# Two projections of a decoder layer turned round: tokens stationary, 512 weight columns moving, and the residual in token rows

## The chip, the cores and the metric

The kernel runs on one core of a Trainium2 chip. The metric is the device time in microseconds of one execution; the time of a kernel is the median of its runs. A core has a matrix engine (TensorE), three engines for elementwise work (VectorE, ScalarE, GpSimd) and a queue engine (SyncE) from which most transfers are issued. TensorE holds up to 128x128 numbers of one operand (the stationary one, loaded by a "weight load") and streams the columns of the other (the moving one) past them; sums are formed in PSUM, in accumulators of 128 rows by up to 512 numbers.

## The reference

One step of a decoder layer for 256 prompt tokens and 8x8 sample tokens, 320 tokens in all, in float32. D = 2048 channels, FF = 5632.

```python
def decoder_layer(x, ...):
    z = rms_norm(x, g_mix) @ w_in
    # z is cut into a gated short convolution (B, C, h), q, k, v and two gates
    ...
    merged = sigmoid(gate_c) * y_conv + sigmoid(gate_a) * y_attn
    h = x + merged @ w_o
    hn = rms_norm(h, g_ffn)
    h = h + (silu(hn @ w_gate) * (hn @ w_up)) @ w_down
    return h, ...
y_prompt, y_sample = rms_norm(hp, g_final), rms_norm(hs, g_final)
```

The change touches `merged @ w_o`, the residual, both norms behind it and `... @ w_down`. The projections w_in, w_conv_out, w_attn_out, w_gate and w_up and the attention stay as they are, up to the form in which their results are handed on.

## The kernel before, in words

**Products in three parts.** TensorE's faster float32 type (fp32r in the rows, printed as f32 in the matmul rows) keeps fewer bits, so each operand is split exactly into a high and a low part, and a product is three matmuls: high weight with high x, high weight with low x, low weight with high x. `load_cols` (L96 to L107) brings a weight tile of four contraction chunks (128 each) by 256 output columns, 512 KB, on SyncE's queue into one of four raw buffers; `split_to` (L92) makes the high part on ScalarE (L93, Copy) and the low part on VectorE (L94, a subtraction), into three buffers each. `product` (L116 to L141) takes these tiles: for two output chunks of 128 channels it holds two accumulators [128 channels, 320 tokens] and issues, for each contraction chunk and output chunk, three matmuls with 128x128 weights stationary and the 320 tokens moving (L132). So everything is kept in [channel, token] form. At the end of each weight tile, `tick()` issues a step of side work (attention, norm pieces) between the matmuls, and what stands in `pending`.

**Order.** Instructions are written in program order and a scheduler puts them in one stream for each engine; `after(...)` forces what is issued in it behind given instructions. Each engine then runs its own stream in order and waits on semaphores.

**Start.** x is loaded in three tiles of token rows (`xs`: 128, 128 and 64 tokens by 2048). `x_prep` (L237 to L250) transposes one chunk of 128 channels with three TensorE transposes (L240; the third is 64 rows by 64), makes the split operands `xh_t` and `xl_t` scaled by g_mix, and copies the chunk to `hT`, the residual in [channel, token] form: 12 such copies on ScalarE (L250), four on VectorE (L248). This stands between the first product, k and v (tile kv). The squares of x are summed from the token rows; `start_rest` (L298 on) spreads the norm's factor (r3, one number for a token) over all 128 rows by a diagonal matrix and a matmul with ones (tile prb, L305; plain float32, two passes each).

**Output projection and second norm (L791 to L831).** Eight products with w_o (tile wo, operands m_h and m_l): each result chunk is added to hT, split into hh_t and hl_t scaled by g_ffn, and its squares are summed on GpSimd into `hacc` (L806 to L810). Behind the first gate product (tile fg) a matmul of ones with hacc (pss2, L830) sums over the channels, and the factor rb2 [128, 320] is worked out from it.

**SwiGLU and down projection (L834 to L891).** FF is worked in two halves, of 24 and 20 chunks. Each half: products with w_gate and w_up (tiles fg, fu), their merge split into a_h and a_l, then eight products with w_down over the half's chunks (tile dn), added to hT (L872). In the second half six transposes behind each product (L878) bring the two finished chunks into token rows, ScalarE sums their squares (L883) and `y_part` (L860) multiplies them by g_final.

**End (L893 to L915).** The last chunk's sum completes the sum of squares, `inv_root` (ScalarE's square root, L181, and a Newton step on VectorE) gives the factor of all three token blocks at once, the rows are scaled in pieces on VectorE and ScalarE, and seven transfers on SyncE's queue write them. A dummy square root (L863) stands ahead of half 1's dn products.

**Tables.** ScalarE loads a table when it changes between kinds of function (ACT_TABLE_LOAD in the rows), Sigmoid and Sqrt among them.

Of the kernel before, what the change touches and what calls it, by code (L numbers as in the profile page):

```python
# [15 lines left out]
D = 2048  # L16
# [24 lines left out]
def hybrid_layer(ctx: ExitStack, tc: tile.TileContext, a: dict, o: list):  # L41
# [50 lines left out]
    def split_to(hi, lo, src):  # L92
        last["hi"] = nc.scalar.activation(hi, src, AF.Copy)  # L93
        last["lo"] = nc.vector.tensor_sub(lo, src, hi.bitcast(F32))  # L94

# [20 lines left out]
    def product(load, nk, xh, xl, name, tiles=None, loaded=None, before=None):  # L116
        """Two output chunks: psum[c][128, T] = sum over nk contraction chunks."""
# [24 lines left out]

    def flip(ap):
# [33 lines left out]
    def inv_root(v, shape, name, pool, out=None):  # L177
        """v ** -0.5, one Newton step on the table's root."""
        s = pool.tile(shape, F32, tag=f"rs_s{shape[1]}", name=u(name))
        r = pool.tile(shape, F32, tag=f"rs_r{shape[1]}", name=u(name))  # L180
# [11 lines left out]
    hT = xp.tile([P, KC, T], F32, name="hT")  # L192
# [22 lines left out]
    xs = [st.tile([P, D], F32, name=f"x{t}") for t in range(3)]  # L215
# [11 lines left out]
    # activity for the PE's clock gate while x is on its way  # L227
# [9 lines left out]
    def x_prep(kc):  # L237
# [9 lines left out]
        if kc % 4 == 3:  # L247
            nc.vector.tensor_copy(hT[:, kc, :], pt[:, :T])  # L248
        else:
            nc.scalar.activation(hT[:, kc, :], pt[:, :T], AF.Copy)  # L250
# [46 lines left out]

    def start_rest():  # L298
        yield
        yield  # L300
        prb = ps_aux("prb")
        for t, (t0, tn) in enumerate(TOK):
            dg = st.tile([P, P], F32, name=f"dg{t}")
            nc.vector.tensor_scalar(dg[:tn, :tn], ident[:tn, :tn], r3[:tn, t:t + 1], None, op0=ALU.mult)
            nc.tensor.matmul(prb[:, t0:t0 + tn], ones[:tn, :], dg[:tn, :tn], start=True, stop=True)  # L305
        nc.vector.tensor_copy(rb, prb[:, :T])
# [90 lines left out]
    def prompt_scores(kv, gp, bias):  # L397
        """Two heads of a kv group; a row of s is [block 0 | block 1 over both key blocks]."""
# [326 lines left out]
    mp_ = ExitStack()  # L725
    mm = mp_.enter_context(tc.tile_pool(name="mm", bufs=1, side="right"))
    m_h = mm.tile([P, KC, T], F32R, name="m_h")
    m_l = mm.tile([P, KC, T], F32R, name="m_l")
    n18 = mm.tile([2 + 2 * NB, DC], F32, name="n18")

    def conv_state():
        for h in range(2):
# [3 lines left out]
            nc.vector.tensor_copy(n18[:, h * 512:(h + 1) * 512], pg[:18, :])  # L736
# [22 lines left out]
    for mp in range(8):  # L759
# [18 lines left out]
        for c in range(2):  # L778
# [3 lines left out]
            split_to(m_h[:, mp * 2 + c, :], m_l[:, mp * 2 + c, :], t)  # L782

# [1 line left out]
    yp.close()  # L785
    hp = ctx.enter_context(tc.tile_pool(name="hp", bufs=1))
    hacc = hp.tile([P, T], F32, name="hacc")
# [3 lines left out]
    for mp in range(8):  # L791
        c0 = mp * CW
        ps = product(
            lambda k0, n: load_cols(w_o, k0, n, c0), KC,
            lambda k: m_h[:, k, :], lambda k: m_l[:, k, :], "wo",
        )
        for c in range(2):
            k = mp * 2 + c
            nc.vector.tensor_add(hT[:, k, :], ps[c][:, :T], hT[:, k, :])
            nc.scalar.activation(hh_t[:, k, :], hT[:, k, :], AF.Copy, scale=g_ffn[:, k:k + 1])  # L800
            nc.vector.scalar_tensor_tensor(
                hl_t[:, k, :], hT[:, k, :], g_ffn[:, k:k + 1], hh_t[:, k, :].bitcast(F32),
                op0=ALU.mult, op1=ALU.subtract,
            )
            if k == 0:
                nc.gpsimd.tensor_tensor(hacc, hT[:, k, :], hT[:, k, :], op=ALU.mult)  # L806
            else:
                t = tmp("tc", "sq")[:, :T]
                nc.gpsimd.tensor_tensor(t, hT[:, k, :], hT[:, k, :], op=ALU.mult)
                nc.gpsimd.tensor_tensor(hacc, hacc, t, op=ALU.add)  # L810
    mp_.close()

# [4 lines left out]
    for half in range(2):  # L817
        f0 = 0 if half == 0 else FH[0]
        nf = FH[half]
        a_h = fp.tile([P, FH[0], T], F32R, tag="ah", name=u("a_h"))  # L820
        a_l = fp.tile([P, FH[0], T], F32R, tag="al", name=u("a_l"))
        for fpair in range(nf // 2):
            c0 = (f0 + fpair * 2) * P
            psg = product(
                lambda k0, n: load_cols(w_g, k0, n, c0), KC,
                lambda k: hh_t[:, k, :], lambda k: hl_t[:, k, :], "fg",
            )
            if half == 0 and fpair == 0:
                pss = ps_aux("pss2")
                nc.tensor.matmul(pss[:, :T], ones, hacc, start=True, stop=True)  # L830
                rstd_of(pss[:, :T], [P, T], "r2", hp, out=rb2)  # L831
            gs = []
            for c in range(2):
                t, t2 = tmp("ta", "gs")[:, :T], tmp("tb", "sg")[:, :T]  # L834
                nc.vector.tensor_mul(t, psg[c][:, :T], rb2)
                nc.scalar.activation(t2, t, AF.Sigmoid)
# [7 lines left out]
            for c in range(2):  # L844
                nc.vector.tensor_mul(gs[c], psu[c][:, :T], gs[c])
                split_to(a_h[:, fpair * 2 + c, :], a_l[:, fpair * 2 + c, :], gs[c])
        if half == 1:
            ya = xp.tile([P, 2, D], F32, tag="xh", name="ya")
            yb = xp.tile([P, 2, D], F32, tag="xl", name="yb")
            y_sb = [ya[:, 0, :], ya[:, 1, :], yb[:, 0, :]]  # L850
            gfb = yb[:, 1, :]
            nc.gpsimd.dma_start(gfb, a["g_final"].partition_broadcast(P))
            ssf = op.tile([P, 3, KC], F32, name="ssf")
            nc.vector.memset(ssf, 1.0)
            s15 = op.tile([P, 3], F32, name="s15")

            def y_part(k, pt):
                for t, (t0, tn) in enumerate(TOK):
                    ks = slice(k * P, (k + 1) * P)
                    nc.vector.tensor_mul(y_sb[t][:tn, ks], pt[:tn, t * P:(t + 1) * P], gfb[:tn, ks])  # L860

            warm = op.tile([P, 1], F32, name="warm")
            nc.scalar.activation(warm, ones[:, 0:1], AF.Sqrt)  # L863
        for mp in range(8):
            c0 = mp * CW
            ps = product(
                lambda k0, n: load_cols(w_d, f0 + k0, n, c0), nf,
                lambda k: a_h[:, k, :], lambda k: a_l[:, k, :], "dn",
            )
            for c in range(2):  # L870
                k = mp * 2 + c
                nc.vector.tensor_add(hT[:, k, :], hT[:, k, :], ps[c][:, :T])  # L872
            if half == 1:
                pc = [ps_aux(u("fa")) for _ in range(2)]
                for c in range(2):
                    k = mp * 2 + c
                    for t, (t0, tn) in enumerate(TOK):
                        nc.tensor.transpose(pc[c][:tn, t * P:(t + 1) * P], hT[:, k, t0:t0 + tn], ident)  # L878
                for c in range(2):
                    k = mp * 2 + c  # L880
                    for t, (t0, tn) in enumerate(TOK):
                        jk = tmp("td", "jk")
                        nc.scalar.activation(  # L883
                            jk[:tn, :P], pc[c][:tn, t * P:(t + 1) * P], AF.Square,
                            accum_out=ssf[:tn, t, k:k + 1],
                        )
                    if k == KC - 2:
                        nc.vector.tensor_reduce(s15, ssf[:, :, 0:KC - 1], axis=AX.X, op=ALU.add)
                        nc.vector.tensor_scalar(s15, s15, 1.0 / D, EPS, op0=ALU.mult, op1=ALU.add)
                    if mp < 7:  # L890
                        y_part(k, pc[c])  # L891

# [1 line left out]
    vf = op.tile([P, 3], F32, name="vf")  # L894
    nc.vector.scalar_tensor_tensor(vf, ssf[:, :, KC - 1], 1.0 / D, s15, op0=ALU.mult, op1=ALU.add)
    rf = inv_root(vf, [P, 3], "rf", op)
    for t, (t0, tn) in enumerate(TOK):
        dst = y_p[0, t0:t0 + tn, :] if t < 2 else y_s.flatten_outer_dims()
        r = rf[:tn, t:t + 1]
        e0 = (KC - 2) * P  # L900
        cuts = (0, 384, 1024, e0) if t == 0 else (0, 1024, e0)
        for i, (a0, a1) in enumerate(zip(cuts[:-1], cuts[1:])):
# [5 lines left out]
            if a1 < e0:  # L908
                nc.sync.dma_start(dst[:, a0:a1], y)
# [47 lines left out]
```

## Time and profile before

The three runs of the kernel took 1718.65 to 1721.42, median 1720.04 us. The profiled execution has a span (first to last instruction) of 1716.3 us; its own time is not listed beside the span.

| stage | from | to | length, us |
|---|---|---|---|
| start, k and v | 0 | 47 | 47 |
| other products of w_in, attention, convolution, gates, merge | 47 | 654 | 607 |
| output projection (wo) | 653.84 | 766.33 | 112.5 |
| gate and up, half 0 | 766.33 | 1104.95 | 338.6 |
| down (dn), half 0 | 1104.95 | 1273.91 | 169.0 |
| gate and up, half 1 | 1273.91 | 1555.3 | 281.4 |
| down (dn), half 1, to its last matmul | 1555.3 | 1700.84 | 145.5 |
| final norm and output | 1700.84 | 1716.3 | 15.4 |

| engine | busy, us | share of the span |
|---|---|---|
| TensorE, matmuls | 1697.9 | 99% |
| TensorE, weight loads | 1678.9 | 98% |
| VectorE | 846.8 | 49% |
| ScalarE | 638.9 | 37% |
| GpSimd | 77.4 | 5% |

A row of an engine's timeline gives start, length, engine, line, operation, and what is written from what; "wo<-m_h,whi" is a matmul into accumulator wo from moving m_h and stationary whi. The busy time of one matmul is longer than the distance between two, since they overlap in the array; the distance between starts is what counts. TensorE's clock was granted in full in every stage but the end (mean 0.997).

### The profile page before, as it was taken

How to read it: one execution, taken by the hardware profiler on the slowest of the kernel's cores; microseconds unless marked ns; L12 is line 12 of the kernel's file. 1: busy time of each engine (PE TensorE's matmuls, PEld its weight loads, DVE VectorE, ACT ScalarE, POOL GpSimd, SP SyncE). 2: the span in 40 equal slices, each digit the busy share in tenths (PEclk: the TensorE clock that was granted, in tenths of full speed). 3: DMA queues.
4: the chain of work that ended last, by engine and by line, in shares of the span. 5: the costliest groups of instructions: out<-in, count | busy, mean ns of one | idle time of the engine just before them, and what ended most of it. 6: DMA issues, size and time to landing. Idle time of an engine off the chain costs nothing.

```text
span 1716.3 us, 27678 instructions
## 1 busy us (share of the span) xinstructions
PE 1697.9 (99%) x11607; PEld 1678.9 (98%) x11607; DVE 846.8 (49%) x1189; ACT 638.9 (37%) x935; POOL 77.4 (5%) x127
## 2 busy tenths in 40 slices
PE   9999999999999999999999999999999999999996
PEld 8999999999999999999999999999999999999996
DVE  5557644544444445555454545433335455554443
ACT  7334433333333333343333333333223333333432
POOL 1101110100000001220000000000000000000000
PEclk9999999999999999999999999999999999999998
DMA  7644444555555444444444444444444445445442
GB/s 205 208 140 137 126 155 148 150 148 150 152 152 148 148 149 149 153 152 148 148 148 152 153 149 148 148 153 153 149 148 148 150 153 152 148 147 172 148 144 90
DMA packets 258813, 258.21 MB, mean 150 GB/s; under 512 B 9138, under 2 KB 255758, under 8 KB 258528
## 3 DMA queue, kind: packets, MB, share of 16 engines
q1 hardware_dynamic: 256384, 250.38, 47.8%
q0 software_dynamic: 2160, 5.93, 1.2%
q8 instruction: 91, 1.49, 0.4%
q14 instruction: 34, 0.28, 0.0%
q10 hardware_dynamic: 144, 0.13, 0.0%
HBM read 253.29 MB, written 5.08 MB: 151 GB/s over the span
## 4 chain that ended last, share of the span: by engine, by line
PE 98%; DMA 1%; ACT 0%; DVE 0%; SPq 0%; issue 0%; DVEq 0%; ACTq 0%
PE dn L132 18%; PE fu L132 18%; PE fg L132 18%; PE wo L132 7%; PE gc L132 7%; PE ga L132 7%; PE C L132 3%; PE H L132 3%; PE B L132 3%; PE q L132 3%; PE ya L132 3%; PE yc L132 3%; PE kv L132 1%; PE ps L405 0%; PE po L469 0%; DMA x<-in_x_sample_dram 0%
## 5 line engine op out<-in xcount | busy, mean ns | idle before, releaser
L94 DVE TENSOR_TENSOR wlo<-wraw,whi 128x1024 fp32r<-128x1024 f32 (+1 forms) x484 | 574.4, 1189 | 717.0 <-ACT whi L93 714.7
L93 ACT ACTIVATE whi<-wraw 128x1024 fp32r<-128x1024 f32 (+1 forms) x484 | 494.4, 1025 | 878.3 <-PE dn L132 198.3
L132 PE MATMUL dn<-a_h,whi 128*128 128x320 f32 x704 | 218.5, 310 | 0.0
L132 PE MATMUL fu<-hh_t,whi 128*128 128x320 f32 x704 | 217.5, 309 | 0.0
L132 PE MATMUL dn<-a_h,wlo 128*128 128x320 f32 x704 | 217.3, 309 | 0.0
L132 PE MATMUL fg<-hl_t,whi 128*128 128x320 f32 x704 | 217.3, 309 | 0.0
L132 PE MATMUL dn<-a_l,whi 128*128 128x320 f32 x704 | 217.3, 309 | 0.0
L132 PE MATMUL fg<-hh_t,wlo 128*128 128x320 f32 x704 | 217.3, 309 | 0.0
L132 PE MATMUL fg<-hh_t,whi 128*128 128x320 f32 x704 | 217.3, 309 | 0.0
L132 PE MATMUL fu<-hl_t,whi 128*128 128x320 f32 x704 | 217.2, 309 | 0.0
L132 PE MATMUL fu<-hh_t,wlo 128*128 128x320 f32 x704 | 217.2, 309 | 0.0
L132 PEld LDWEIGHTS fu<-hh_t,whi 128*128 128x128 f32 x704 | 132.2, 188 | 0.1
L132 PEld LDWEIGHTS fu<-hl_t,whi 128*128 128x128 f32 x704 | 132.2, 188 | 0.1
L132 PEld LDWEIGHTS dn<-a_l,whi 128*128 128x128 f32 x704 | 132.3, 188 | 0.0
L132 PEld LDWEIGHTS fu<-hh_t,wlo 128*128 128x128 f32 x704 | 132.2, 188 | 0.0
L132 PEld LDWEIGHTS dn<-a_h,whi 128*128 128x128 f32 x704 | 132.2, 188 | 0.0
L132 PEld LDWEIGHTS fg<-hh_t,whi 128*128 128x128 f32 x704 | 132.2, 188 | 0.0
L132 PEld LDWEIGHTS dn<-a_h,wlo 128*128 128x128 f32 x704 | 132.2, 188 | 0.0
L132 PEld LDWEIGHTS fg<-hh_t,wlo 128*128 128x128 f32 x704 | 132.2, 188 | 0.0
L132 PEld LDWEIGHTS fg<-hl_t,whi 128*128 128x128 f32 x704 | 132.2, 188 | 0.0
L132 PE MATMUL gc<-xh_t,whi 128*128 128x320 f32 x256 | 79.6, 311 | 0.0
L132 PE MATMUL ga<-xh_t,whi 128*128 128x320 f32 x256 | 79.4, 310 | 0.0
(260 smaller groups left out, 2919.9 us busy)
## 6 DMA issues: line engine op xcount, KB each, us to landing
wraw<-in_w_in_dram SPq DMA_DIRECT2D x116, 512.0 KB, 3.7
wraw<-in_w_gate_dram SPq DMA_DIRECT2D x88, 512.0 KB, 3.6
wraw<-in_w_up_dram SPq DMA_DIRECT2D x88, 512.0 KB, 3.6
wraw<-in_w_down_dram SPq DMA_DIRECT2D x88, 512.0 KB, 3.5
wraw<-in_w_o_dram SPq DMA_DIRECT2D x32, 512.0 KB, 3.5
wraw<-in_w_in_dram SPq DMA_DIRECT2D x40, 256.0 KB, 4.4
wraw<-in_w_conv_out_dram SPq DMA_DIRECT2D x16, 512.0 KB, 3.5
wraw<-in_w_attn_out_dram SPq DMA_DIRECT2D x32, 256.0 KB, 4.0
```

Of the source, the lines that this page charges most:

```text
L93: last["hi"] = nc.scalar.activation(hi, src, AF.Copy)
L94: last["lo"] = nc.vector.tensor_sub(lo, src, hi.bitcast(F32))
L132: last["mm"] = nc.tensor.matmul(ps[c][:, :T], w[:, k, c * P:(c + 1) * P], x(kc), start=(kc == 0 and i == 0), stop=(kc == nk - 1 and i == 2),)
```

## The change

Four things change together.

1. Output and down projection go through `token_product`: the activations are stationary (128 tokens) and 512 weight columns move. A weight tile, `load_rows`, is two contraction chunks by 512 columns, 512 KB as before. A chunk takes eight matmuls: three for each of two token blocks of 128, and two for the 64 sample tokens, whose high and low parts lie side by side in one stationary operand of 128 columns (accumulator rows 0 to 63 and 64 to 127, added up later). The result is [token, channel], 512 channels at a time. The merged activations are handed on in one tile, m_hl and a_hl, with high and low parts ordered for this (`split_tokens`, three instructions for two).
2. The residual stays in the token rows `xs` for the whole kernel; hT and its copies at the start are gone. `add_tokens` adds an accumulator set with four VectorE instructions, `squares` sums squares on ScalarE, 512 wide.
3. The second norm's operand is transposed from the token rows (`h_prep`, three transposes a chunk) as side work in the wo products, and for the last four chunks ahead of the first gate product. The norm's factor is spread by `spread`, as at the start.
4. The final norm is done on token rows, one block of tokens after the other, each with its own root, with g_final multiplied in ahead for three quarters of the columns; six output transfers. The dummy square root is forced behind the last sigmoid. The convolution state is assembled in a raw weight buffer.

```diff
+    def load_rows(w, k0, n, c0):
+        raw = wp.tile([P, KT // 2, CN], F32, tag="wraw", name=u("wraw"), bufs=4)
+        nc.sync.dma_start(
+            raw[:, :n, :], w[k0 * P:(k0 + n) * P, c0:c0 + CN].rearrange("(k p) n -> p k n", p=P)
+        )
+        hi = wp.tile([P, KT // 2, CN], F32R, tag="whi", name=u("whi"), bufs=3)
+        lo = wp.tile([P, KT // 2, CN], F32R, tag="wlo", name=u("wlo"), bufs=3)
+        split_to(hi[:, :n, :], lo[:, :n, :], raw[:, :n, :])
+        return hi, lo
...
+    def token_product(load, nk, hl, name):
+        ps = [ps_acc(u(name)), ps_acc(u(name)), ps_aux(u(name))]
+        step = KT // 2
+        for k0 in range(0, nk, step):
+            n = min(step, nk - k0)
+            hi, lo = load(k0, n)
+            todo = []
+            for k in range(n):
+                kc = k0 + k
+                for t, (t0, tn) in enumerate(TOK[:2]):
+                    h, l = hl[:, kc, t0:t0 + tn], hl[:, kc, LOW + t0:LOW + t0 + tn]
+                    todo += [(t, kc, k, h, hi, kc == 0), (t, kc, k, l, hi, False), (t, kc, k, h, lo, False)]
+                both = hl[:, kc, TP:LOW]
+                todo += [(2, kc, k, both, hi, kc == 0), (2, kc, k, both, lo, False)]
+            if k0 + n == nk:
+                todo.sort(key=lambda x: x[0])
+            for t, kc, k, x, w, first in todo:
+                end = kc == nk - 1 and w is lo
+                last["mm"] = nc.tensor.matmul(ps[t], x, w[:, k, :], start=first, stop=end)
...
+    def split_tokens(hl, src):
+        nc.scalar.activation(hl[:, 0:T], src, AF.Copy)
+        nc.vector.tensor_sub(hl[:, T:LOW], src[:, TP:T], hl[:, TP:T].bitcast(F32))
+        nc.vector.tensor_sub(hl[:, LOW:2 * T], src[:, :TP], hl[:, :TP].bitcast(F32))
+
+    def add_tokens(dst, ps, cs):
+        for t in range(2):
+            nc.vector.tensor_add(dst[t][:, cs], ps[t], dst[t][:, cs])
+        for half in range(2):
+            nc.vector.tensor_add(dst[2][:64, cs], ps[2][half * 64:(half + 1) * 64, :], dst[2][:64, cs])
...
-        if kc % 4 == 3:
-            nc.vector.tensor_copy(hT[:, kc, :], pt[:, :T])
-        else:
-            nc.scalar.activation(hT[:, kc, :], pt[:, :T], AF.Copy)
...
+    def spread(r, out, pool):
+        prb = ps_aux(u("prb"))
+        for t, (t0, tn) in enumerate(TOK):
+            dg = pool.tile([P, P], F32, tag=f"dg{t}", name=u("dg"))
+            nc.vector.tensor_scalar(dg[:tn, :tn], ident[:tn, :tn], r[:tn, t:t + 1], None, op0=ALU.mult)
+            nc.tensor.matmul(prb[:, t0:t0 + tn], ones[:tn, :], dg[:tn, :tn], start=True, stop=True)
+        nc.vector.tensor_copy(out, prb[:, :T])
...
-    n18 = mm.tile([2 + 2 * NB, DC], F32, name="n18")
+        n18 = raw_tile().rearrange("p k n -> p (k n)")
...
-            split_to(m_h[:, mp * 2 + c, :], m_l[:, mp * 2 + c, :], t)
+            split_tokens(m_hl[:, mp * 2 + c, :], t)
...
+    def squares(out, cs, i):
+        for t, (t0, tn) in enumerate(TOK):
+            junk = wk.tile([P, 512], F32, tag="junk", name=u("junk"), bufs=1)
+            nc.scalar.activation(junk[:tn, :], xs[t][:tn, cs], AF.Square, accum_out=out[:tn, t, i:i + 1])
+
+    def h_prep(k):
+        pt = ps_aux(u("ht"))
+        for t, (t0, tn) in enumerate(TOK):
+            nc.tensor.transpose(pt[:, t0:t0 + tn], xs[t][:tn, k * P:(k + 1) * P], ident[:tn, :tn])
+        nc.scalar.activation(hh_t[:, k, :], pt[:, :T], AF.Copy, scale=g_ffn[:, k:k + 1])
+        nc.vector.scalar_tensor_tensor(hl_t[:, k, :], pt[:, :T], g_ffn[:, k:k + 1], ...)
...
-    for mp in range(8):
-        ps = product(lambda k0, n: load_cols(w_o, k0, n, c0), KC, ..., "wo")
-            nc.vector.tensor_add(hT[:, k, :], ps[c][:, :T], hT[:, k, :])
-            ... hh_t, hl_t, hacc ...
+    for nb in range(4):
+        cs = slice(nb * CN, (nb + 1) * CN)
+        ps = token_product(lambda k0, n: load_rows(w_o, k0, n, nb * CN), KC, m_hl, "wo")
+        add_tokens(xs, ps, cs)
+        squares(ssh, cs, nb)
+        done.append(nb)
...
-                pss = ps_aux("pss2")
-                nc.tensor.matmul(pss[:, :T], ones, hacc, start=True, stop=True)
-                rstd_of(pss[:, :T], [P, T], "r2", hp, out=rb2)
+                nc.vector.tensor_reduce(s2, ssh, axis=AX.X, op=ALU.add)
+                r2 = rstd_of(s2, [P, 3], "r2", hp)
+                spread(r2, rb2, hp)
...
+            with after(last["sig"]):
+                nc.scalar.activation(warm, ones[:, 0:1], AF.Sqrt)
+        for nb in range(4):
+            cs = slice(nb * CN, (nb + 1) * CN)
+            ps = token_product(lambda k0, n: load_rows(w_d, f0 + k0, n, nb * CN), nf, a_hl, "dn")
+            add_tokens(xs, ps, cs)
             if half == 1:
-                ... six transposes, squares and y_part for two chunks ...
+                squares(ssf, cs, nb)
+                if nb < 3:
                     for t, (t0, tn) in enumerate(TOK):
+                        nc.vector.tensor_mul(xs[t][:tn, cs], xs[t][:tn, cs], gfb[:tn, cs])
...
+    e0 = 3 * CN
     for t, (t0, tn) in enumerate(TOK):
+        nc.vector.tensor_reduce(sf[:tn], ssf[:tn, t, :], axis=AX.X, op=ALU.add)
+        nc.vector.tensor_scalar(sf[:tn], sf[:tn], 1.0 / D, EPS, op0=ALU.mult, op1=ALU.add)
+        r = inv_root(sf, [P, 1], "rf", op, rows=tn)[:tn]
+        nc.vector.scalar_tensor_tensor(y[:tn, e0:D], y[:tn, e0:D], r, gfb[:tn, e0:D], op0=ALU.mult, op1=ALU.mult)
+        nc.scalar.activation(y[:tn, 0:CN], y[:tn, 0:CN], AF.Copy, scale=r)
+        nc.vector.tensor_scalar(y[:tn, CN:e0], y[:tn, CN:e0], r, None, op0=ALU.mult)
+        nc.sync.dma_start(dst[:, 0:CN], y[:tn, 0:CN])
+        nc.sync.dma_start(dst[:, CN:D], y[:tn, CN:D])
```

More of the change, by code (lines that the diff above doesn't have):

```diff
@@ L175, in rstd_of, with inv_root @@
         return inv_root(v, shape, name, pool, out)
-    def inv_root(v, shape, name, pool, out=None):
-        s = pool.tile(shape, F32, tag=f"rs_s{shape[1]}", name=u(name))
-        r = pool.tile(shape, F32, tag=f"rs_r{shape[1]}", name=u(name))
+    def inv_root(v, shape, name, pool, out=None, rows=P):
+        v = v[:rows]
+        s = pool.tile(shape, F32, tag=f"rs_s{shape[1]}", name=u(name), bufs=3)[:rows]
+        r = pool.tile(shape, F32, tag=f"rs_r{shape[1]}", name=u(name), bufs=3)[:rows]
         nc.scalar.activation(s, v, AF.Sqrt)
@@ L191, in hybrid_layer @@
     xl_t = xp.tile([P, KC, T], F32R, tag="xl", name="xl_t")
-    hT = xp.tile([P, KC, T], F32, name="hT")
+    xs = [xp.tile([P, D], F32, name=f"x{t}") for t in range(3)]
     e_scr = dr.tile([NH, EL], F32, name="e_scr")
@@ L300, in start_rest @@
         yield
[L301 to L306, printed above, removed]
+        spread(r3, rb, st)
         nc.vector.tensor_scalar(rbq, rb, HD ** -0.5, None, op0=ALU.mult)
@@ L790, in hybrid_layer @@
     hl_t = xp.tile([P, KC, T], F32R, tag="xl", name="hl_t")
-    for mp in range(8):
[L792 to L795, printed above, removed]
-        )
-        for c in range(2):
-            k = mp * 2 + c
-            nc.vector.tensor_add(hT[:, k, :], ps[c][:, :T], hT[:, k, :])
[L800 to L810, printed above, removed]
+    ssh = hp.tile([P, 3, 4], F32, name="ssh")
@@ new lines, in h_parts @@
+    def h_parts():
+        for nb in range(4):
+            while len(done) <= nb:
+                yield
+            for k in range(nb * 4, nb * 4 + 4):
+                h_prep(k)
+                yield
+    done = []
+    left = sum(1 for _ in side_work[0])
+    assert left == 0, left
+    side_work[0] = h_parts()
+    for nb in range(4):
[4 more added lines that the diff above has]
+        done.append(nb)
@@ L811, in hybrid_layer, with h_before @@
     mp_.close()
+    side_work[0] = None
+    def h_before(k):
+        if k < 4:
+            h_prep(12 + k)
     fp = ctx.enter_context(tc.tile_pool(name="fp", bufs=1))
@@ L819, in hybrid_layer @@
         nf = FH[half]
-        a_h = fp.tile([P, FH[0], T], F32R, tag="ah", name=u("a_h"))
-        a_l = fp.tile([P, FH[0], T], F32R, tag="al", name=u("a_l"))
+        a_hl = fp.tile([P, FH[0], 2 * T], F32R, tag="ahl", name=u("a_hl"))
         for fpair in range(nf // 2):
             c0 = (f0 + fpair * 2) * P
+            first = half == 0 and fpair == 0
             psg = product(
                 lambda k0, n: load_cols(w_g, k0, n, c0), KC,
-                lambda k: hh_t[:, k, :], lambda k: hl_t[:, k, :], "fg",
+                lambda k: hh_t[:, k, :], lambda k: hl_t[:, k, :], "fg", before=h_before if first else None,
             )
-            if half == 0 and fpair == 0:
-                pss = ps_aux("pss2")
-                nc.tensor.matmul(pss[:, :T], ones, hacc, start=True, stop=True)
-                rstd_of(pss[:, :T], [P, T], "r2", hp, out=rb2)
+            if first:
+                s2 = hp.tile([P, 3], F32, name="s2")
+                nc.vector.tensor_reduce(s2, ssh, axis=AX.X, op=ALU.add)
+                r2 = rstd_of(s2, [P, 3], "r2", hp)
+                spread(r2, rb2, hp)
             gs = []
@@ L844, in hybrid_layer @@
             for c in range(2):
+                k = fpair * 2 + c
                 nc.vector.tensor_mul(gs[c], psu[c][:, :T], gs[c])
-                split_to(a_h[:, fpair * 2 + c, :], a_l[:, fpair * 2 + c, :], gs[c])
+                split_tokens(a_hl[:, k, :], gs[c])
         if half == 1:
[L848 to L851, printed above, removed]
+            gfb = xp.tile([P, D], F32, tag="xh", name="gfb")
@@ L863, in hybrid_layer @@
[L863 to L872, printed above, removed]
+            ssf = op.tile([P, 3, 4], F32, name="ssf")
+            warm = op.tile([P, 1], F32, name="warm")
@@ L877, in hybrid_layer @@
                     for t, (t0, tn) in enumerate(TOK):
[L878 to L891, printed above, removed]
```

53 lines of the change are left out of this document (17 added, 36 removed).

## The prediction

> **What bounds the kernel now.** I read the page first (span, busy shares, slices, chain), then the chain in order of time for the interval between matmuls, then the groups by shape, then short stretches of the timeline. All times are microseconds.
>
> ```profile
> span 1716.3 us, 27678 instructions
> PE 1697.9 (99%) x11607; PEld 1678.9 (98%) x11607; DVE 846.8 (49%) x1189; ACT 638.9 (37%) x935; POOL 77.4 (5%) x127
> PE 98%; DMA 1%; ACT 0%; DVE 0%; SPq 0%; issue 0%; DVEq 0%; ACTq 0%
> ```
>
> TensorE carries 98% of the chain, VectorE and ScalarE are less than half busy. So only two things count: what TensorE's stream costs, and the few places where it waits (start, second norm, end).
>
> ```profile
> 653.84 112.65 PE wo L132 x768
> 851.51 14.08 PE fg L132 x96
> 1104.95 168.96 PE dn L132 x1152
> 1574.24 17.16 PE dn L132 x117
> 1592.53 17.17 PE dn L132 x117
> ```
>
> The chain in order of time (start, length, engine, tile, line, count) gives the real interval: 14.08/96 = 112.65/768 = 168.96/1152 = 0.14667 for each 128x320 matmul, without a gap. The 309 ns that the groups show for one matmul overlap. The changed products are 768 (wo) and 2112 (dn: 88 loads of 24), 2880 matmuls, 422.4 of the span.
>
> **The products.** Each contraction chunk and 512 output columns cost 12 matmuls of 320 moving columns (4 column chunks x 3); now 8 of 512 (two token blocks x 3, and 2 for the sample tokens, whose high and low parts stand side by side in one stationary operand). That makes 1920 matmuls; the columns streamed rise from 3840 to 4096 a chunk, 6.7%. Gain or loss thus hangs on what a matmul costs beside its columns. No row has a 512-column matmul of this type; three stretches bound it.
>
> ```profile
> 1.06 3.78 PE L230 MATMUL wm<-ones 128*128 128x128 f32 x16 [1.06 <-DVE ones L156]
> 10.28 0.47 PE L132 MATMUL kv<-xh_t,whi 128*128 128x320 f32 x1
> 10.54 0.47 PE L132 MATMUL kv<-xl_t,whi 128*128 128x320 f32 x1
> 10.81 0.47 PE L132 MATMUL kv<-xh_t,wlo 128*128 128x320 f32 x1
> 160.66 0.38 PE L409 MATMUL ps<-kT,q_sb 64*128 64x128 f32 x2
> 160.88 0.59 PE L405 MATMUL ps<-kT,q_sb 64*128 64x256 f32 x2
> 161.32 0.38 PE L409 MATMUL ps<-kT,q_sb 64*128 64x128 f32 x2
> ```
>
> At the start the clock is still low: the 128-column passes of plain float32 come every (3.78-0.42)/15 = 0.22, later every 0.11, half. The split type's 320 columns take 0.267 there (10.28, 10.54, 10.81). Halved, that is 0.1333, but the steady interval is 0.1467: 13.3 ns do not follow the clock. Either they come once a matmul (512/320 x 0.1333 + 0.0133 = 0.2267) or they grow with the columns (0.1467 x 1.6 = 0.2347). The low end is 0.2133 (columns alone), and close above it stands the 256-column plain pass, 0.44/2 = 0.2175 to 0.22 in full clock, which takes two cycles a column (at the low clock 0.22/128 is twice 0.267/320) and so as many as 512 single ones. I take 0.2267: the interval is 0.14667 to the last digit over hundreds of matmuls, an extra of exactly a tenth has no reason of its own in 320 columns, and an unscaled start cost that a slow clock hides has one. So 1920 x 0.2267 = 435.2 against 422.4: **+12.8**, ends -12.8 and +28.2.
>
> One page weighs in on the other side. The Trainium skill, "TensorE: Matmul & The Clock Gate", section "Back-to-back issue gap", gives a warm gap of N/2.4 + 2.5 ns. For 320 columns that is 135.8 ns, against 146.7 here, so the trace does not bear it out for this type. By it a 512-column matmul is 215.8 ns, the term -8.1, and the whole change a gain of some 5.5.
>
> **The transposes.** The last residual no longer needs its 48 transposes (L878), the second norm's input now needs 48 (three for each of 16 chunks, h_prep). In half 1 of dn, a period of 18.29 (1592.53-1574.24) less 120 x 0.14667 = 17.60 leaves 0.69 for two chunks, 0.345 each; 14 lie in the stream: 4.8. The new ones have the form of the start's: the third is 64 rows by 64 columns.
>
> ```profile
> 16.87 0.58 PE L240 MATMUL pt<-ident,x 128*128 128x128 f32 x3
> 18.36 0.58 PE L240 MATMUL pt<-ident,x 128*128 128x128 f32 x3
> ```
>
> There a chunk's period is 1.49, less six products 0.88: 0.61 each, 9.8 for 16. **+5.0**; the low end, should they cost 0.345, is +0.7. In the built order they stand after whole weight tiles, the first one 16 matmuls (3.6) behind the end of the product that they read; for the last four, two transposes of chunk 12 stand ahead of the first fg matmul and wait for the token block's sum, some 0.2, within the rounding.
>
> **The second norm's scale.** Two 320-column float32 passes give way to six small ones after fg's first product.
>
> ```profile
> 780.41 0.70 PE L830 MATMUL pss<-hacc,ones 128*128 128x320 f32 x2
> 781.09 0.31 PE L132 MATMUL fu<-hl_t,whi 128*128 128x320 f32 x1
> 46.08 1.05 PE L305 MATMUL prb<-dg,ones 128*128 128x128 f32 x6 [1.18 <-DVE dg L304]
> 47.05 0.41 PE L132 MATMUL kv<-xh_t,whi 128*128 128x320 f32 x1
> ```
>
> The old pair holds the stream 781.09-780.41, less one fu product of 0.147, = 0.53; the six, by the same form at the start, 0.97 and 0.10 for the late next one, 1.07: **+0.5**. Their operand comes from a chain of short VectorE and ScalarE steps that stands in the middle of fg (14 long), so they find it ready; the square sums leave GpSimd, where nothing waited.
>
> **The start.** x stays in token rows, so the 16 copies into hT (12 on ScalarE) go.
>
> ```profile
> 34.65 0.41 PE L132 MATMUL kv<-xh_t,wlo 128*128 128x320 f32 x1 [0.34 <-DVE wlo L94]
> 28.37 0.43 ACT L250 ACTIVATE hT<-pt 128x320 f32<-128x320 f32 x1
> 41.91 1.28 ACT L181 ACT_TABLE_LOAD   x1
> 44.59 0.31 PE L132 MATMUL kv<-xh_t,wlo 128*128 128x320 f32 x1
> ```
>
> TensorE waits twice: 0.65-0.15 = 0.5 before 34.65, and from 44.59 to 46.08, 1.34 beyond an interval, for the first norm's root. ScalarE runs without a gap from 28.4 to 41 and each copy holds it about 0.31; in the built order three more squares stand ahead of the last chunk, so the root's table load comes some 2 earlier and the operand before 44.7. **-1.85**, ends 0 and -1.85.
>
> **The end.**
>
> ```profile
> 1700.84 0.31 PE L132 MATMUL dn<-a_h,wlo 128*128 128x320 f32 x1
> 1703.27 1.28 ACT L181 ACT_TABLE_LOAD   x1
> 1708.82 0.60 DVE L912 SCALAR_TENSOR_TENSOR yb<-fa,rf,yb 64x128 f32<-64x128 f32 x2
> 1710.41 1.22 SPq L915 DMA_DIRECT2D out_dram<-yb  x1
> out_dram<-yb SPq DMA_DIRECT2D x2, 256.0 KB, 4.7
> out_dram<-ya SPq DMA_DIRECT2D x1, 320.0 KB, 2.4
> ```
>
> From the last dn matmul to the end of the span are 15.4. The root's table load goes: the built order has it ahead of half 1's dn, and no other behind it. In its place stand four 512-wide sums (0.69 each, next fence), squares, and three norms one behind the other instead of one. Followed through the built order, with 0.43 from a matmul's start to its reader: block 0 is summed at -1.2 and squared at -0.3, block 1 at 0.2 and 1.1, the sample rows by 2.3; the three roots come at 3.0, 5.7 and 7.9 (each five short VectorE steps of 0.16 to 0.2, queued behind the former block's 0.7 and 0.75 of scaling), the last rows are scaled at 9.3, their 384 KB land about 4 later, and 1.1 follows as now. 14.4: **-1.0**, ends -3 and +3.
>
> **What I cost at nothing, and its cover.**
>
> ```profile
> L94 DVE TENSOR_TENSOR wlo<-wraw,whi 128x1024 fp32r<-128x1024 f32 x444 | 548.1, 1234 | 699.7 <-ACT whi L93 697.5
> L94 DVE TENSOR_TENSOR wlo<-wraw,whi 128x512 fp32r<-128x512 f32 x40 | 26.2, 687 | 17.3 <-ACT whi L93 17.3
> L872 DVE TENSOR_TENSOR hT<-hT,dn 128x320 f32<-128x320 f32 x32 | 15.5, 485 | 22.8 <-PE dn L132 22.8
> wraw<-in_w_down_dram SPq DMA_DIRECT2D x88, 512.0 KB, 3.5
> ```
>
> A weight tile keeps its 512 KB (120 loads on SP's queue as before, 2 KB runs for 1 KB), its 1.23 split and its turn on TensorE: 16 x 0.2267 = 3.63 for 24 x 0.1467 = 3.52, above the 3.5 of a landing, with several tiles in flight. At each of 12 product ends VectorE does four sums of about 0.69 (a 512-wide one takes 0.687), and the third next tile's split queues behind: 2.8 + 1.2 = 4.0. The order puts two tiles' splits ahead, 7.25 of matmuls, so this is covered. One more short subtraction for each of 60 chunks, 24 squares, nine multiplications by g_final and the added transposes' copies fall to engines that idle half the time. The convolution state borrows one of four weight buffers; the load that waits for it on SP is nine loads later. Were that cover gone, 3.5 + 1.0 + 1.2 would be paid once.
>
> **Sum.** 12.8 + 5.0 + 0.5 - 1.85 - 1.0 = +15.45 on a profiled span of 1716.3: 1731.75. What lies around the span (the profiled execution's own time is not listed; the median is 3.7 above its span) stays: 1720.04 + 15.45 = **1735.5**.
>
> **Rivals.**
> - *The 13.3 ns grow with the columns.* For it: a read that cannot keep up with the full clock would look the same at one size. 1920 x 0.2347 = 450.6, +28.2, with the other +2.65: 1750.9.
> - *The extra is a wait for weights, hidden under longer columns; the change is faster.* Place: between every two products. Price: an interval between 0.2133 and 0.2175, middle 0.2154, 413.6, -8.8; in all -6.15, 1713.9. It decides below 0.2186, where products and the +2.65 cancel. For it: the weight loads are 98% busy, and the low clock's 0.267 shows no extra, as it would if the two ran side by side. Against: the loads of the 128-column float32 passes are as long, and those passes come every 0.11.
>
> ```profile
> L409 PEld LDWEIGHTS ps<-kT,q_sb 64*128 64x128 f32 x32 | 6.0, 187 | 0.9
> L132 PEld LDWEIGHTS dn<-a_h,whi 128*128 128x128 f32 x704 | 132.2, 188 | 0.0
> ```
>
> - *The sums at product ends hold TensorE*, if the two tiles are not split ahead: up to 4.0 - 3.63 and a start, about 1 each, +12: 1747. Against: the order, and whi's idle time, which is a wait for free buffers, not for data.
>
> **Chances.** Forecast 0.68, proportional 0.12, faster rival 0.14, held sums 0.06. The likeliest case alone spans 1729 (transposes +0.7, end -3) to 1744 (start 0, end +3, 3 of small stalls). With the two slower rivals 1729 to 1752, 0.86 less the forecast's own tails. A measurement here tells about 0.2% (3.4) from no change: the faster rival gives faster 0.10 and same 0.04, the forecast's edge same 0.01; slower 0.85.
>
> **What would show it.** The chain in order of time: wo 512 matmuls in 116.1 plus 7.4 of transposes, dn of the first half 768 in 174.1; at 166 or below the faster rival is right, at 180 the proportional one. The two early waits gone from the start; no table load behind the last dn matmul; roots there at three places. I am wrong if the interval is not 0.2267, or if TensorE shows idle time at product ends.

## The result

The changed kernel takes 1741.14 us (median of four runs, 1741.08 to 1741.82) against 1720.16 before: 1.0125 of the time, 95% interval 1.011 to 1.0139. It is slower by 21.0, where 15.45 were forecast. The profiled execution has a span of 1739.4 us, 23.1 above that of before.

The page and the chain of the changed kernel:

```profile
span 1739.4 us, 25691 instructions
PE 1720.6 (99%) x10651; PEld 1617.3 (93%) x10651; DVE 847.1 (49%) x1224; ACT 636.1 (37%) x877; POOL 44.8 (3%) x96
PE 98%; DVE 1%; DMA 0%; ACT 0%; SPq 0%; issue 0%; DVEq 0%
```

TensorE is still the bound. It runs 956 matmuls fewer and is busy 22.7 longer. The chain of the changed kernel in order of time (start, length, engine, tile, line, count) shows where:

```profile
50.79 3.72 PE q L146 x24
654.27 33.60 PE wo L180 x144
688.29 3.93 PE wo L180 x16
692.64 3.92 PE wo L180 x16
781.36 0.88 PE fg L146 x6
797.37 0.81 PE prb L357 x6
798.17 14.28 PE fu L146 x96
1122.21 175.81 PE dn L180 x768
1579.62 145.60 PE dn L180 x636
```

dn runs without a gap at 175.81/768 = 0.2289 a matmul, wo at 33.60/144 = 0.2333: two intervals for the same instruction, both above the 0.2267 of the forecast. From one wo row to the next lie 692.64 - 688.29 = 4.35, of which sixteen matmuls are 3.73; the rest, 0.62, is one group of three transposes. The first q product of the kernel before begins at 51.95:

```profile
51.95 3.72 PE q L132 x24
```

The stages, each from the start of its first row in the chain, in the kernel before and in the changed one:

| stage | before | after | difference | forecast |
|---|---|---|---|---|
| start, to the first q product | 51.95 | 50.79 | -1.2 | -1.85 |
| q to wo | 601.9 | 603.5 | +1.6 | 0 |
| wo and its transposes | 112.7 | 127.1 | +14.4 | +10.8 |
| first fg to dn | 338.5 | 340.9 | +2.4 | +3.0 |
| dn, half 0 | 169.0 | 175.8 | +6.9 | +5.1 |
| gate and up, half 1 | 281.6 | 281.6 | 0 | 0 |
| dn, half 1, to its last matmul | 145.3 | 146.1 | +0.8 | -0.5 |
| end | 15.4 | 13.7 | -1.7 | -1.0 |
| sum | 1716.3 | 1739.4 | +23.1 | +15.5 |

Between the span and the listed time lie 1.8 in this kernel and about as much in the runs below; before's profile, whose own time was not listed, was thus of an execution near 1718.1, two below the median. So 2.1 of the 23.1 do not show in the medians.

The timeline of VectorE in the changed kernel holds the one new wait, in the first gate product:

```profile
317.88 0.68 DVE L792 COPY wraw<-pg 18x512 f32<-18x512 f32 x1 [2.30 <-PE pg L791]
318.49 3.47 DVE L94 TENSOR_TENSOR wlo<-wraw,whi 128x1024 fp32r<-128x1024 f32 x3
```

VectorE waits 2.30 for the transposes of the convolution state (pg), and three weight splits stand behind that copy. The chain names the first of them ahead of the resumed product:

```profile
313.89 3.52 PE gc L146 x24
318.49 1.21 DVE wlo L94
319.75 3.20 PE gc L146 x20
```

### The profile page after: what moved, and what is told of

Read it like the earlier page. It is cut to its first block, busy times and chain, and to the rows that moved or that the text cites. A ratio compares the mean times of both kernels' runs of the same rounds, so it can differ in the third digit from the quotient of the medians.

```text
span 1739.4 us, 25691 instructions
## 1 busy us (share of the span) xinstructions
PE 1720.6 (99%) x10651; PEld 1617.3 (93%) x10651; DVE 847.1 (49%) x1224; ACT 636.1 (37%) x877; POOL 44.8 (3%) x96
## 4 chain that ended last, share of the span: by engine, by line
PE 98%; DVE 1%; DMA 0%; ACT 0%; SPq 0%; issue 0%; DVEq 0%
PE dn L180 18%; PE fg L146 18%; PE fu L146 18%; PE wo L180 7%; PE ga L146 6%; PE gc L146 6%; PE C L146 3%; PE H L146 3%; PE B L146 3%; PE q L146 3%; PE ya L146 3%; PE yc L146 3%; PE kv L146 2%; PE ps L462 0%; PE ht L857 0%; DMA x<-in_x_sample_dram 0%
## 5 line engine op out<-in xcount | busy, mean ns | idle before, releaser
L93 ACT ACTIVATE whi<-wraw 128x1024 fp32r<-128x1024 f32 (+1 forms) x484 | 494.0, 1024 | 891.9 <-PE dn L180 188.9
L180 PE MATMUL dn<-whi,a_hl 128*128 128x512 f32 x880 | 287.3, 391 | 0.0
L180 PE MATMUL dn<-wlo,a_hl 128*128 128x512 f32 x528 | 206.6, 391 | 0.0
L180 PEld LDWEIGHTS dn<-whi,a_hl 128*128 128x128 f32 x880 | 165.2, 188 | 36.0
L180 PEld LDWEIGHTS dn<-wlo,a_hl 128*128 128x128 f32 x528 | 99.2, 188 | 21.7
L180 PE MATMUL wo<-whi,m_hl 128*128 128x512 f32 x320 | 107.0, 399 | 0.0
L146 PE MATMUL gc<-xh_t,wlo 128*128 128x320 f32 x256 | 79.3, 310 | 1.3 <-DVE wlo L94 1.3
```

The costliest lines, as they stand in the source:

```text
L146: last["mm"] = nc.tensor.matmul(ps[c][:, :T], w[:, k, c * P:(c + 1) * P], x(kc), start=(kc == 0 and i == 0), stop=(kc == nk - 1 and i == 2),)
L180: last["mm"] = nc.tensor.matmul(ps[t], x, w[:, k, :], start=first, stop=end)
```

## The experiments

In all of them "extra" is what a matmul costs beside its columns.

**What a matmul of the split type costs.** Behind the last product of the changed kernel stands a stretch of TensorE work on its own operands, 30 matmuls of a kind, one kind after the other. The cut shows the loop of one kind, with names for the numbers that vary:

```diff
+    mst = mb.tile([P, 1024], F32R, name="mst")
+    mmv = mb.tile([P, 1024], F32R, name="mmv")
...
+        for i in range(MR):
+            o = shift + i % 3 * 128
+            nc.tensor.matmul(pm[:m, :n], mst[:, o:o + m], mmv[:, mshift:mshift + n], start=i == 0, stop=i == MR - 1)
```

> The changed kernel with a stretch of 37 kinds of matmul, 30 of each, behind the last product; the other engines are idle there. It varies the moving columns (128 to 512), the place of either operand in memory by 4 to 1024 bytes, and the stationary columns (32 to 128). Fixed extra of 13.3 ns a matmul (the prediction's law): 0.1467 at 320 and 0.2267 at 512 moving columns here, wherever the operands lie; the 0.2289 of dn and 0.2333 of wo would then be 2 and 7 ns of disturbance by the other engines. Extra that grows with the columns: 0.2347 at 512, 0.176 at 384. Extra set by the stationary operand (how it lies in memory, how many columns it has): at 512 columns the interval moves by several ns with the stationary shift of 32 bytes or with 32 or 64 stationary columns, and not with the moving shift, and the extra is about the same for 256 and 512 moving columns.

The chain of this run, 30 matmuls a row:

```profile
1728.45 3.30 PE pm L962 x30
1731.75 3.38 PE pm L967 x30
1735.13 3.62 PE pm L972 x30
1738.75 4.40 PE pm L977 x30
1743.15 5.20 PE pm L982 x30
1748.35 6.20 PE pm L987 x30
1754.55 6.86 PE pm L992 x30
1782.18 7.00 PE pm L1012 x30
1796.14 6.80 PE pm L1022 x30
1802.94 7.10 PE pm L1027 x30
1823.96 6.88 PE pm L1042 x30
1844.66 6.81 PE pm L1057 x30
1855.87 4.40 PE pm L1067 x30
1864.67 4.40 PE pm L1077 x30
1880.42 4.30 PE pm L1092 x30
1925.03 4.08 PE pm L1132 x30
```

The first seven rows are 128, 192, 256, 320, 384, 448 and 512 moving columns: 0.110, 0.113, 0.121, 0.1467, 0.1733, 0.2067 and 0.2287. From 320 to 384 columns the interval grows by 0.0267, 0.417 ns a column, so that 320 columns alone are 0.1333 and 0.0133 are left; at 384 the same 0.0133 (0.1733 - 0.16). The extra does not grow with the columns up to 384; at 448 it is 0.020, and at 512 it is 0.0133 in the best rows: L1022 and L1057, with the stationary operand 256 or the moving one 1024 bytes further, give 6.80/30 and 6.81/30 = 0.227. The row without a shift (L992, 0.2287) comes to the same: by the starts in its trace its first ten intervals change between 0.224 and 0.236, and from the eleventh on they are 0.2267. Below 256 columns the interval stops falling, near 0.11; these short rows ran beside the last steps of the final norm. So the fixed extra of the forecast is there.

But at 512 columns it is a floor: with the stationary operand 64 bytes further (L1012) the interval is 0.2333, with the moving one 64 bytes further (L1042) 0.2293, and neither settles; VectorE and ScalarE are idle from 1736 on. At 320 columns the same shifts change nothing: 0.1467 in L977, L1067 and L1077. With 32 stationary columns instead of 128 they take 0.1433 (L1092), so here the number of stationary columns sets 3 ns of the extra at most. What lies where in memory thus costs up to 10 ns at 512 columns (0.2367 in L1027, with the moving operand 4 bytes further) and nothing at 320; at 448 it was not varied.

The growing extra (0.2347 wherever the operands lie, 0.176 at 384) is out, and so is an extra that other engines cause.

**wo moved in memory.** In the changed kernel's memory, by the layout of its tiles (no profile prints it), the weight tiles begin 320 bytes behind a multiple of 512, wo's stationary operand 480 and dn's 0. One pad moves wo's operand:

```diff
     m_hl = mm.tile([P, KC, 2 * T], F32R, name="m_hl")
+    m_pad = mm.tile([P, 120], F32, name="m_pad")
+    nc.vector.memset(m_pad, 0.0)
```

> The changed kernel with the merged activations (stationary operand of wo) 480 bytes lower in memory, so that they begin on a multiple of 512 bytes as those of dn do. If the place of the stationary operand sets the extra: wo at 0.2289 a matmul instead of 0.2333, the wo stage 2.3 us shorter, dn unchanged. If other engines' work in that stage or the number of chunks does: wo stays at 0.2333 within 0.0005.

```profile
654.56 32.98 PE wo L180 x144
1120.40 175.81 PE dn L180 x768
```

wo is at 32.98/144 = 0.2290, the value of dn, and dn is as it was. So the place of the stationary operand makes the difference between the two; the stage and its number of chunks do not.

**Both placed.** Pads of 160 and 320 bytes bring both operands to 320 behind a multiple of 512, like the weights.

```diff
     m_hl = mm.tile([P, KC, 2 * T], F32R, name="m_hl")
+    m_pad = mm.tile([P, 40], F32, name="m_pad")
+    nc.gpsimd.memset(m_pad, 0.0)
...
+    f_pad = fp.tile([P, 80], F32, name="f_pad")
+    nc.gpsimd.memset(f_pad, 0.0)
...
         a_hl = fp.tile([P, FH[0], 2 * T], F32R, tag="ahl", name=u("a_hl"))
```

> The changed kernel with both stationary operands moved so that they begin 320 bytes behind a multiple of 512, as the weight tiles do (the distance between the operands that gave 0.2267 in the measuring stretch); nothing else differs. If the extra over 0.2267 comes from the distance between the two operands in memory: wo and dn both at 0.2267, -3.4 and -3.1 against the changed kernel, 1734.6 in all, which is the prediction's own sum less 0.9. If only a start on a multiple of 64 bytes counts: both stay at 0.2289, 1738.9. If the other engines' work adds the 2.2 of dn: the same.

```profile
654.50 32.66 PE wo L180 x144
1119.63 174.10 PE dn L180 x768
```

dn is at 174.10/768 = 0.2267, to the digit the forecast's interval and its 174.1 for half 0; wo is at 0.2268 in its first product. Behind each group of transposes its first intervals are longer again, so that wo as a whole is 2.8 shorter, not 3.4. The time is 1735.8 (ratio to before 1.0096, 1.0083 to 1.011), 5.3 below the changed kernel; 1734.6 was expected.

**The convolution state in memory of its own.** The changed kernel, with the borrowed weight buffer given back:

```diff
-        n18 = raw_tile().rearrange("p k n -> p (k n)")
+        n18 = [mm.tile([18, 512], F32, name="n18"), wk.tile([P, 512], F32, tag="junk", name=u("n18"), bufs=1)]
...
```

> The changed kernel with the convolution state assembled in memory of its own instead of a borrowed weight buffer. If the borrowed buffer moved the split of a weight tile behind the wait for the state's transposes: the wait of 1.6 at the first gate product (at 318 us) goes, all later stages begin about 1.5 us earlier, the rest is unchanged. If it was a late transfer: the wait stays at 1 us or more.

```profile
314.62 3.52 PE gc L146 x24
318.14 0.44 PE pg L791 x4
318.57 3.52 PE gc L146 x24
```

The second piece of gc follows the transposes at once, as in the kernel before; from the first q to the first wo it takes 653.42 - 51.52 = 601.9, as before, instead of 603.5. In VectorE's order two splits that stood behind the state's copy stand ahead of it again. The one time taken, 1740.39, is only 0.75 below the changed kernel's median: its first q begins at 51.52 instead of 50.79.

**Start and end alone, on the kernel before.**

```diff
-        if kc % 4 == 3:
-            nc.vector.tensor_copy(hT[:, kc, :], pt[:, :T])
-        else:
-            nc.scalar.activation(hT[:, kc, :], pt[:, :T], AF.Copy)
+        nc.vector.tensor_copy(hT[:, kc, :], pt[:, :T])
...
-            nc.scalar.activation(warm, ones[:, 0:1], AF.Sqrt)
+            with after(last["sig"]):
+                nc.scalar.activation(warm, ones[:, 0:1], AF.Sqrt)
```

> The kernel before with two pieces of the change alone, both products left as they are: the residual's copies at the start all on VectorE, none on ScalarE, and the dummy square root forced behind the last sigmoid. By the prediction's terms: the wait for the root at 46 us goes and that at 34.65 shrinks (-1.85 at most), and the table load at the end goes (-1.28): 1717 us against 1720, at the edge of what can be told. If the start is bound by the arrival of x, or if VectorE's twelve more copies delay the split, the start gives nothing: 1718.8.

1717.57 against 1719.26, ratio 0.9989 (0.998 to 0.9998). That is 1.7 less, where 3.1 were expected of both terms and 1.3 of the end alone: the time does not tell the two apart. The chain of its start:

```profile
29.09 15.45 PE kv L132 x104
44.54 0.81 PE prb L302 x6
45.35 3.72 PE kv L132 x24
```

104 matmuls run through to prb without either wait: from the first kv product to the first q it takes 40.4 instead of 42.6. The end shrinks from 15.4 to 14.3 behind the last product. Both terms hold in this trace, which is of the fastest of eleven executions (1715.2 to 1720.2). Taken once more, beside the last run below:

> The kernel before with the change's start and end once more, beside the run with 128-row transposes: 1717.6 as measured. The difference of the two on one chip is what the shorter groups are worth at the start: 4.3 if TensorE's stream is all that counts there, less than 1 if it isn't.

1716.59 against 1719.70, ratio 0.9981 (0.9973 to 0.999), 3.1 less. This profile is of the slowest execution, 1720.03, and shows what else moves the start:

```profile
20.21 3.21 PE kv L132 x12
33.89 15.44 PE kv L132 x104
```

Twelve kv products take 3.21 at 20 us here, 0.267 each; in the profile of the first run twelve take 1.76 from 17.06 on, 0.147 each. TensorE goes over to the short interval at about 15 us there and at about 24 here. So from the first kv product to the first q it takes 43.4 here, more than in the kernel before, and x brings the first product at 11.5 instead of 9.7: together that is the 4.8 between the two spans.

The granted clock of the first run is 0.50 from 10 to 14 us. For this run and the kernel before it reads 1.00 there, though the interval was 0.267: at the start the interval is the better witness. The start's gain can thus be read only from executions that go over equally soon. The kernel before (at 14.1), the changed kernel (14.4) and the first run (14.9) go over 4.5 to 5.2 behind their first product, so these three can be compared.

**The groups of three transposes.** The changed kernel, placed, with the state in its own memory, and with 128 rows for the sample tokens' transposes, at the start and in h_prep:

```diff
+    nc.gpsimd.memset(xs[2][64:, :], 0.0)
...
-            nc.tensor.transpose(pt[:, t0:t0 + tn], xs[t][:tn, k * P:(k + 1) * P], ident[:tn, :tn])
+            nc.tensor.transpose(pt[:, t0:t0 + P], xs[t][:, k * P:(k + 1) * P], ident)
```

> The changed kernel placed as in the run before, with the convolution state in memory of its own, and with every transpose of the sample tokens (start and second norm) taking 128 rows, 64 of them zeros, so that no transpose changes the number of rows. If the change of rows sets the 0.61 of a group of three (0.109 for each transpose and about 0.09 on either side of the 64-row one): 0.345 a group, 32 groups, -8.5, together with -1.6 and -6.5: 1724.5. If the wait lies in what follows a transpose, a group stays at 0.61: 1733.

```profile
682.91 3.66 PE wo L180 x16
686.58 0.33 PE ht L863 x3
686.90 3.67 PE wo L180 x16
```

A group now takes 0.33 and the 16 matmuls behind it 3.66, 0.04 over 16 x 0.2267: 0.37 instead of 0.62. So a short transpose among full ones costs some 0.25. By the starts in the trace of the changed kernel, 0.20 lie between the second transpose and the short one and 0.20 between it and the next product, where 0.11 and 0.03 lie in this run. Two short ones in a row, which stand once in fg (at 782.69), lie 0.11 apart, like two full ones. That points to the change of rows as what costs, and not to the short form. The Trainium skill says, on the page "TensorEngine Tiling (Array Packing)", section "Key Properties", that changing the tiling mode drains TensorE; these starts agree that something of the kind is paid, about 0.09 ahead of the short transpose and 0.17 behind it.

The time is 1727.59, ratio 1.0046 (1.0031 to 1.0061): 13.5 below the changed kernel, 3 less than expected. 1.2 were already missing in the placed run; at the start TensorE waits 1.75 for a split of x (ahead of 10.53; the next run shows why) and 0.5 for one of the weights (ahead of 32.13), and the shorter groups gave less than the 4.3 counted.

**The same start on the kernel before.**

> The kernel before with its products, with the change's start and end (copies off ScalarE, dummy root behind the last sigmoid) and the sample tokens' transposes at the start with 128 rows. If the change of rows sets the price of a group: 16 x 0.27 = -4.3 beside the -1.7 to -3 of start and end: 1713. If the start is bound by the arrival of the weights or their split instead: 1717, as without it.

1714.0, ratio 0.9965 (0.9953 to 0.9978). That is 1.0 above the number expected, and not for the reason given: the time from the first kv product to the first q is 40.8, no less than without the shorter groups. The chain shows why:

```profile
4.77 6.12 DMA sink_bc<-in_sinks_dram
10.91 0.04 DVE nsink L314
11.00 0.56 DVE xl_t L243
11.59 1.70 PE kv L132 x5
```

The zeros on GpSimd changed the order of VectorE's stream: a small step (nsink) that waits for a load came ahead of the first split of x, and TensorE waited 2.5. With the zeros written by VectorE that order is as before:

```diff
-    nc.gpsimd.memset(xs[2][64:, :], 0.0)
+    nc.vector.memset(xs[2][64:, :], 0.0)
```

> As the run before on the kernel before (its products, the change's start and end, 128-row transposes at the start), but the zeros for the 64 unused rows are written by VectorE instead of GpSimd, which leaves the small loads at the start, and a VectorE step that waits for one of them, where they were. In the run before TensorE waited 2.5 us for that step at 9 to 11.6 us. If that wait hid the gain of the shorter groups: 2 to 2.5 below that run, 1711.5 to 1712. If VectorE and ScalarE bound the start in its place: 1714 again.

1713.4, ratio 0.996 (0.9946 to 0.9973). Each beside its own runs of the kernel before, this is 6.3 less and the former run 5.8, so that the wait for the small step was worth some 0.5, no more than runs of one kernel differ by, and not the 2 to 2.5 expected. In the profile of this run the first product waits for x instead, 7.50 after the last issue:

```profile
3.44 7.50 DMA x<-in_x_sample_dram
16.78 0.33 PE pt L241 x3
17.11 0.88 PE kv L132 x6
29.35 13.98 PE kv L132 x92
```

It is 3.2 below the run without the shorter groups on the same chip, between the two values named ahead of it. A group takes 0.33 here too, against about 0.6 in the first run. But nine of the 48 transposes, three groups of the 16, stand ahead of the first product, where TensorE waits for x anyway. That leaves 13 groups, by estimate 13 x 0.27 = 3.5. The chain goes through VectorE and ScalarE from 23 to 29 us, but TensorE's one clear wait there is 0.3, ahead of 29.35. This kernel, the old products with the change's start and end and full-height transposes, is 0.4% faster than the kernel before.

## Why the prediction was right, and where it was not

Slower, in the range and by the mechanism named: the direction came out of the fixed extra, and the time 5.6 above the forecast. The interval itself missed: by the prediction's own sign ("I am wrong if the interval is not 0.2267") its main term was wrong in size. And the time missed by less than the sum of the span, 5.6 against 7.7, because an error in what lies around the span went the other way; that part was luck.

- *Products, +12.8.* The law was right (0.0133 fixed: 0.1467, 0.1733 and 0.2267), the sum was too small: 512 x 0.2333 + 1408 x 0.2289 = 441.8, +19.4. The step that failed is the term of 0.2267 itself, sized too small because it was taken as the interval wherever operands lie; it is the floor, and where the changed kernel's operands lie, dn takes 2.2 and wo 6.7 ns more. Placing them gave the 0.2267. This is 6.6 of the 7.7 by which the span exceeded the sum.
- *The two rivals on the interval.* Growth with the columns would be 0.176 at 384 columns; 0.1733 was measured. "The extra is a wait for weights": then 256 columns would take as long as 320; they take 0.121. A shortest interval there is, near 0.11, but at 128 and 192 columns only. The Trainium skill's gap, N/2.4 + 2.5 ns ("TensorE: Matmul & The Clock Gate", section "Back-to-back issue gap"), fits bf16 here, 4.08/30 = 0.136 at 320 columns, and not this type.
- *Transposes, +5.0.* Right: 0.62 in wo where 0.61 was taken; the four groups in fg add 16.0 - 14.1 = 1.9 and two of their transposes 0.2 ahead of it. Less the 4.8 saved, that is 4.7.
- *Second norm, +0.5.* Right: 0.81 for prb and 0.20 for the next product's late begin, 1.0 against 1.07.
- *Start, -1.85.* Right in mechanism: neither of the two waits is there, and first kv to first q is 40.8 instead of 42.6, -1.8. Only -1.2 show, since x came 0.6 later.
- *End, -1.0.* Right in sign, 0.7 too small: the three norms overlap better than followed. The rows answer to the roots named at 3.0, 5.7 and 7.9:

```profile
1728.26 0.75 DVE L952 SCALAR_TENSOR_TENSOR x<-x,rf,gfb 128x512 f32<-128x512 f32 x1
1730.36 0.75 DVE L952 SCALAR_TENSOR_TENSOR x<-x,rf,gfb 128x512 f32<-128x512 f32 x1
1732.24 0.74 DVE L952 SCALAR_TENSOR_TENSOR x<-x,rf,gfb 64x512 f32<-64x512 f32 x1
```

  that is 2.5, 4.6 and 6.5 behind the last matmul (1725.73), and no table load stands among them.
- *Costed at nothing: the borrowed buffer.* Wrong. The step said that the load that waits for it is nine loads later; the load was not late. The built order put the state's copy, which waits for TensorE, ahead of a split that TensorE needed: 1.6.
- *Sums at product ends.* The cover held: 768 dn matmuls in 175.81 are 768 steady intervals, over four product ends.
- *Around the span.* The forecast carried 3.7 over from the median; 1.8 would have been right, which would have put the forecast at 1733.5. The terms above leave less than half a us of the 7.7 unexplained.

What stays open is by which rule the place of the operands sets the interval. In the stretch, no shift, 256 bytes either way and 1024 settled at 0.2267, but so did the stationary operand 16 bytes further (L1002, 6.81/30) and not the moving one (L1032, 6.94/30); 4, 32, 64 and 128 bytes gave 0.229 to 0.237. The starts of dn repeat 0.226, 0.229 and 0.232, as those of L1042 do, and its operands lie 320 bytes apart, 64 more than 256: this fits a distance that counts modulo 256, but does not show it. No run tells which part of the memory makes the difference.

## What to carry to other kernels

Fewer and longer matmuls pay only by the fixed part of each, here 13 ns for the split float32 type: count the columns as well. Here 6.7% more of them are 61440 columns, 25.6 at 0.417 ns each, against 12.8 for 960 such parts saved. Before trusting the interval of a new shape, measure it with the operands where the kernel has them, and try to move them. A buffer that is lent, or a step put on another engine, can change the order of instructions far from it; read the built order around every wait. Compare the starts of two kernels between executions in which TensorE goes over to its short interval equally soon.

## What was not expected of the hardware

At 512 moving columns the interval of the split type depends on where the operands lie (0.2267 to 0.2333 in the kernels; 7.10/30 = 0.237 in the stretch with the moving operand 4 bytes further, L1027), at 320 it does not. A transpose of 64 rows between ones of 128 costs about 0.25 more than one of 128 rows with half of them zeros. One execution of a kernel kept to 0.267 a matmul until about 15 us, another of the same kernel until about 24, which by its start is 3 us of the time.
